# A causal convolution on TensorE: other buffers for the results of the first two steps, and one mid weight by ScalarE and an accumulating DMA

## The chip, the cores and the metric

The kernel runs on one core of a Trainium2 chip. The metric is the device time of one execution in microseconds (us). The kernel before took 785.68 us (median of three runs, 783.73 to 785.83). The profiled execution took 783.4 us, of which the profile covers a span of 781.4 us. All times in views of the profile count from the start of that span.

## The reference

The reference is a causal convolution over time with a full matrix for each tap. x has shape 8 x 4096 x 512 (batch, time, features), the kernel has 8 taps of 512 x 512, and everything is float32.

```
out = np.zeros_like(x)
for k in range(K):                       # K = 8
    shifted = x if k == 0 else concatenate([zeros(B, k, D), x[:, :-k, :]], axis=1)
    out += np.matmul(shifted, kernel[k])
```

So each output row is the sum of eight products of a row of x (the present one and its seven predecessors) with a matrix.

## The kernel before

**Tiling.** The 32768 rows are cut into 128 runs of 256 rows, one run for each partition. A step takes 8 rows of each run, so there are 32 steps (`NIT`). x is loaded in halves of four rows (`load_x(i, h)`, GpSimd's DMA queue, float32 cast to bf16 into two buffers `xin`) and brought into the transposed form that TensorE needs in `XT`. In the steady part this is done by a DMA transpose (`transpose_x`, SyncE's queue), in the first two steps partly by TensorE (`transpose_pe`).

**Fewer products.** Eight outputs from eight taps would take 64 products of a 128 x 512 tile with a 512 x 512 matrix. The kernel splits taps and rows into halves three times. Each half is LO or HI, and a third combination, MID, uses the difference of the two weights and serves both halves. The weights lie in tiles `W[a, b, c]`, all named `w`. The eight loaded ones have no MID in their index; the others are differences formed on the way, by `mid_dve(level, u, v)`, a VectorE subtraction of 128 x 2048 elements in bf16. The sums of x rows that stand opposite these weights are formed by VectorE in tiles whose names begin with D (`D1`, `D2`, `D4`, `D41`, `D42`, `D421`, ...).

**Nodes.** The unit of work is a node: a step i and an outermost index a. A node has nine products (`product`, four matmuls each, L190): `node_a1`, `node_a0`, `node_u`, two `node_v`, four `node_l`. Between them ScalarE and VectorE carry partial sums from one PSUM tile to the next: `node_seed` (L249, L251: ScalarE copies, one negated), `node_dts` (L255, ScalarE), `node_d` (L265 and L76, VectorE). The last part, `node_e`, takes a finished pair of rows (128 x 1024, float32) out of PSUM. For a MID node this is a ScalarE copy into a tile `ms` (L292), the mid sum; for LO and HI nodes it is a VectorE addition or subtraction of the mid sum, into a tile `y`, followed by a store on SyncE's queue (`store`, L275).

**The first two steps** go in another order, since the weights are still being loaded: (0, LO), (1, LO), (0, HI), (1, HI), (0, MID), (1, MID), numbered 0 to 5. Node 0 is computed without differences, by sixteen products `direct(m, t)`. The results of nodes 0 to 3 are copied by ScalarE (L288) into buffers, where they wait for the mid sums: `node_y` (VectorE) adds the mid sum of node 4 or 5 into them in place, and then they are stored. These buffers come from the pools of the later steps: `y` with four tiles, `ms` with two, and `f` with two. From node 6 on, each step has nodes MID, LO, HI in this order.

**What sets the order.** The schedule is written by hand: each engine executes its instructions in the order in which the program text names them, and the program text of the first two steps is one long list (L337 to L559). Waits between engines follow from which tiles are read and written. A tile of a pool with n buffers is taken again for the (n+1)-th request, and the new writer waits for everything that used the old content, a store too.

Of the kernel before, what the change touches and what calls it, by code (L numbers as in the profile page):

```python
# [18 lines left out]
LO, HI, MID = 0, 1, 2  # L19
# [3 lines left out]
def kernel(  # L23
# [6 lines left out]
    nc = tc.nc  # L30
# [10 lines left out]
    ADD = mybir.AluOpType.add  # L41
# [14 lines left out]
    W = {}  # L56
# [11 lines left out]
    D21 = spool.tile([P, 4, D], bf, name="D21")  # L68
# [3 lines left out]
    F0 = spool.tile([P, D], bf, name="F0")  # L72
    A1 = spool.tile([P, 2, D], bf, name="A1")

    def tt(o, a, b, op):
        nc.vector.tensor_tensor(out=o, in0=a, in1=b, op=op)  # L76


    def load(out, src):
        nc.gpsimd.dma_start(out=out, in_=src)  # L80
# [3 lines left out]
    def load_x(i, h):  # L84
        xin[i, h] = xpool.tile([P, 4, D], bf, name="xin")
        load(xin[i, h], xr[:, K * i + 4 * h:K * i + 4 * h + 4, :])

    def transpose_x(i, h):
        nc.sync.dma_start_transpose(
            out=XT[:, 4 * h:4 * h + 4, :].rearrange("p j (c m) -> p (j c) m", m=P),  # L90
            in_=xin[i, h].rearrange("p j d -> p (j d)"))
# [20 lines left out]
    def prep_d41(h):  # L112
        if h == LO:
            tt(D41[:, 0:2], D4[:, 7::-7], D4[:, 0:2], ADD)
        else:
            tt(D41[:, 2:4], D4[:, 3:5], D4[:, 4:6], ADD)
# [7 lines left out]
    def prep_d421(h):  # L124
        if h == LO:
            tt(D421[:, 0:4:2], D42[:, 7:0:-6], D42[:, 0:4:2], ADD)
            tt(D421[:, 1:4:2], D42[:, 0:4:2], D42[:, 1:4:2], ADD)
        else:
            tt(D421[:, 4:8], D42[:, 3:7], D42[:, 4:8], ADD)
# [5 lines left out]
    def pair(k):  # L135
        return ppool.tile([P, 2, D], f32, name=f"pp{k}")
# [4 lines left out]
    H, HF = XT, D421.bitcast(f32).rearrange("p (t b) d -> p t (b d)", b=2)  # L141
# [6 lines left out]
    def load_w(tap):  # L148
        n = K - 1 - tap
        load(W[n >> 2, n >> 1 & 1, n & 1], kr[:, :, tap, :])  # L150

    def mid(level, u, v):

        if level == 0:
            return W[MID, u, v], W[HI, u, v], W[LO, u, v]
        if level == 1:
            return W[u, MID, v], W[u, HI, v], W[u, LO, v]
        return W[u, v, MID], W[u, v, LO], W[u, v, HI]

    def mid_dve(*which):  # L160
        o, u, v = mid(*which)
        tt(o, u, v, SUB)

    load_w(4)
    load(H[:, 1:4], xr[:, RUN - 7:RUN - 4, :])
    ident = spool.tile([P, P], bf, name="ident")
# [8 lines left out]
    def transpose_pe(name, k, src, t0, t1):  # L175
        o = pair(k).bitcast(bf).rearrange("p a (b d) -> p (a b) d", b=2)
        for t in range(t0, t1):
            for c in range(DC):
                nc.tensor.transpose(o[:, t - t0, c * P:(c + 1) * P], src[:, t, c * P:(c + 1) * P],  # L179
                                    ident)  # L180
        bank[name] = o[:, 0:t1 - t0]
# [3 lines left out]
    XF = D42  # L185


    def product(bank, comp, w, start):
        for c in range(DC):
            nc.tensor.matmul(bank, lhsT=comp[:, c * P:(c + 1) * P], rhs=w[:, c, :],  # L190
                             start=start and c == 0, stop=c == DC - 1,
                             skip_group_check=True)

    mpool = ctx.enter_context(tc.tile_pool(name="m", bufs=2))
    cpool = ctx.enter_context(tc.tile_pool(name="c", bufs=2))
    fpool = ctx.enter_context(tc.tile_pool(name="f", bufs=2))
    ypool = ctx.enter_context(tc.tile_pool(name="y", bufs=4))
# [31 lines left out]
    def node_a1(k):  # L229
        n = Node()  # L230
        nodes.append(n)
        n.k, (n.i, n.a) = k, order[k]
        a = n.a
        n.s = streams(n.i, a)
        n.q = pair(3)
        product(n.q[:, 1], n.s[1][1], W[a, MID, HI], True)
        nc.scalar.copy(out=n.q[:, 0], in_=n.q[:, 1])  # L237
        n.p = {}
# [4 lines left out]
    def node_u(n):  # L243
        product(n.q[:, 1], n.s[0], W[n.a, MID, MID], False)

    def node_seed(n, b_):
        n.p[b_] = pair((2 * n.k + b_) % 3)
        if b_ == LO:
            nc.scalar.copy(out=n.p[b_][:, 1], in_=n.q[:, 1])  # L249
        else:  # L250
            nc.scalar.mul(out=n.p[b_][:, 1], in_=n.q[:, 1], mul=-1.0)  # L251
# [8 lines left out]
    def node_d(n, b_):  # L260
        p = n.p[b_]
        if b_ == LO:
            tt(p[:, 0], n.dts, p[:, 1], SUB)
        else:
            nc.vector.scalar_tensor_tensor(out=p[:, 0], in0=p[:, 1], scalar=-1.0,  # L265
                                           in1=n.dts, op0=MUL, op1=SUB)

    ms = {}

    def node_l(n, b_, j):  # L270
        product(n.p[b_][:, j], n.s[3][2 * b_ + j], W[n.a, b_, j], False)

    def store(i, a, b_, y):
        t0 = K * i + 4 * a + 2 * b_
        nc.sync.dma_start(out=orr[:, t0:t0 + 2, :], in_=y)  # L275
# [7 lines left out]
    def node_e(n, b_):  # L283
        p = n.p[b_]
        if n.k < 4:
            pool, name = ((ypool, "y"), (mpool, "ms"), (ypool, "y"), (fpool, "f"))[n.k]
            y = pool.tile([P, 2, D], f32, name=name)
            nc.scalar.copy(out=y, in_=p)  # L288
            first[n.i, n.a, b_] = y
        elif n.a == MID:  # L290
            ms[b_] = mpool.tile([P, 2, D], f32, name="ms")
            nc.scalar.copy(out=ms[b_], in_=p)  # L292
        else:
            y = ypool.tile([P, 2, D], f32, name="y")
            if b_ == HI and n.k == len(order) - 1:

                for j, eng in enumerate((nc.scalar, nc.sync)):
                    tt(y[:, j], p[:, j], ms[b_][:, j], ADD if n.a == LO else SUB)
                    eng.dma_start(out=orr[:, K * n.i + 4 * n.a + 2 * b_ + j, :], in_=y[:, j])
            else:  # L300
                tt(y, p, ms[b_], ADD if n.a == LO else SUB)
                store(n.i, n.a, b_, y)
# [12 lines left out]
    def direct(m, t):  # L315
        n = K // 2 - 1 - m
        product(n0.p[t // 2][:, t % 2], D4[:, t - m] if t >= m else E4[:, 4 + t - m],
                W[LO, n >> 1, n & 1], m == 0)


    C0, C1 = W[MID, HI, MID], W[MID, LO, MID]

    def to(z):
        return z.rearrange("p t (c m) -> p t c m", m=P)[:, :, :, 1:P]

    def prev(z):
        return z.rearrange("p t (c m) -> p t c m", m=P)[:, :, :, 0:P - 1]

    def first_run(z):

        nc.vector.memset(z[:, :, 0:D:G], 0.0)
# [2 lines left out]

    nc.vector.tensor_copy(out=H[:, 4:6], in_=HF[:, 0:2])  # L337
    nc.scalar.copy(out=H[:, 6:8], in_=HF[:, 2:4])
    n0.p = {0: pair(0), 1: pair(1)}
    load_w(6)  # L340
# [21 lines left out]
    load_x(1, 0)  # L362
    tt(to(E4[:, 1:4]), prev(bank["he"]), to(XF[:, 1:4]), ADD)
    direct(2, 2)
    direct(0, 1)
    first_run(E4[:, 1:4])
    direct(1, 1)
    tt(D1, XF[:, 3:5], XF[:, 4:6], ADD)
    mid_dve(1, LO, HI)
    nc.vector.tensor_copy(out=F0, in_=XF[:, 4])  # L370
    mid_dve(2, LO, HI)
    tt(F21, D2[:, 0:4], D2[:, 1:5], ADD)
    direct(2, 0)
# [5 lines left out]
    direct(2, 3)  # L379
    mid_dve(2, LO, MID)  # L380
    direct(1, 0)
    transpose_pe("x1", 2, xin[0, 1], 0, 4)
    nc.vector.tensor_copy(out=XT[:, 4:8], in_=bank["x1"])  # L383
    tt(D4[:, 4:8], XF[:, 4:8], XT[:, 4:8], ADD)
    direct(1, 2)
    tt(D42[:, 3], D4[:, 1], D4[:, 3], ADD)
    transpose_pe("x2", 2, xin[1, 0], 0, 4)
    prep_d41(HI)
    direct(3, 2)
# [10 lines left out]
    tt(D41[:, 1], T4[:, 0], T4[:, 1], ADD)  # L400
    load_w(3)
    node_a1(1)
    direct(2, 1)
    node_u(nodes[1])
    tt(D41[:, 0], D4[:, 7], T4[:, 0], ADD)
    tt(T42[:, 0:2], D4[:, 6:8], T4[:, 0:2], ADD)
# [2 lines left out]
    mid_dve(1, HI, HI)  # L409
    load_w(1)  # L410
    node_e(nodes[0], 0)
    load_x(1, 1)
    load_x(2, 0)
# [8 lines left out]
    node_seed(nodes[1], 1)  # L422
    mid_dve(1, HI, LO)
    node_e(nodes[0], 1)
    mid_dve(2, HI, HI)
    node_v(nodes[1], 1)
    mid_dve(2, HI, MID)
    node_l(nodes[1], 0, HI)
    load_x(2, 1)
    node_d(nodes[1], 1)  # L430
    prep_d421(HI)
    mid_dve(0, HI, HI)
    node_a1(2)
    node_l(nodes[1], 0, LO)
    node_e(nodes[1], 0)
    transpose_x(1, 1)
    node_a0(nodes[2])
# [24 lines left out]
    node_u(nodes[3])  # L462
    node_seed(nodes[3], 0)
    node_l(nodes[2], 1, HI)
    mid_dve(0, HI, LO)
    node_seed(nodes[3], 1)
    tt(D421[:, 0:4], D42[:, 3:7], D42[:, 4:8], ADD)
    node_e(nodes[2], 1)
# [14 lines left out]
    node_dts(nodes[4])  # L483
    tt(D21[:, 2:4], C1[:, 0:2], C1[:, 2:4], ADD)
    mid_dve(2, MID, MID)
    tt(D21[:, 0:2], C0[:, 0:2], C1[:, 0:2], ADD)
    tt(A1[:, 1], C1[:, 0], C1[:, 1], ADD)
    load_x(3, 0)
    transpose_x(2, 0)
    mid_dve(2, MID, LO)  # L490
    node_e(nodes[3], 0)
# [148 lines left out]
```

## Time and profile before

| | before |
|---|---|
| time, median of 3 | 785.68 us |
| span of the profile | 781.4 us |
| TensorE busy | 761.4 us (97%) |
| VectorE busy | 659.6 us (84%) |
| ScalarE busy | 281.9 us (36%) |
| GpSimd busy | 41.3 us (5%) |
| one VectorE subtraction of weights (128 x 2048 bf16) | 1218 ns, 19 of them |
| one ScalarE copy of 128 x 2048 bf16 (L394) | 1912 ns |
| load of half a step of x, issue to landing | 5.7 us median |
| store of a `y` tile / of an `ms` tile, issue to landing | 3.4 / 8.4 us median |

Busy time of PE is modelled at the ends of matmuls, and shapes of one line are averaged unless they are kept apart. Because the steady part from step 2 on repeats every three nodes (23.3 us), views of the first 110 us have to be read by themselves: averages over the span say nothing of them. In the views, `pp` are the PSUM tiles, PE is TensorE's matmul, PEld its weight load, DVE is VectorE, ACT is ScalarE, POOL is GpSimd and SPq is the queue of SyncE. L76 is the line of a helper through which all VectorE additions and subtractions run; they are told apart by their tiles. An arrow with a line in brackets names what ended the wait just before the instruction.

### The profile page before, as it was taken

To read this page: it belongs to the slowest core of one execution; us is meant where nothing else is said; L and a number is where in the kernel's file an instruction comes from. 1 tells how busy PE (TensorE), PEld (TensorE's weight loads), DVE (VectorE), ACT (ScalarE), POOL (GpSimd) and SP (SyncE) were. 2 spreads that over 40 slices of the span, in tenths; PEclk is the share of its full clock that TensorE was granted. 3 is DMA by queue.
4 is the path that set the end of the run, shared out by engine and by line. 5 is a ranking of instruction groups with operands and counts; after the bars stand their busy time and mean duration, and the time that the engine had idled before them with its cause. 6 is when DMAs were issued, how large, how long until landed. Compare 5 with 4: busy or idle time off the path is not lost.

```text
span 781.4 us, 9358 instructions
## 1 busy us (share of the span) xinstructions
PE 761.4 (97%) x3505; PEld 346.3 (44%) x3576; DVE 659.6 (84%) x768; ACT 281.9 (36%) x460; POOL 41.3 (5%) x79
## 2 busy tenths in 40 slices
PE   7899899999999999999999999999999999999997
PEld 3444344444444444444444444444444444444443
DVE  4999888888888888888898888888888898888895
ACT  2453333333333333333323343333333333343332
POOL 4000000000000000000000000000000000000000
PEclk9999999999999999999999999999999999999999
DMA  9974878776877787777687787778797867678843
GB/s 200 211 122 137 203 178 207 159 193 163 184 170 195 177 189 170 181 181 195 155 198 173 174 186 191 190 163 181 167 193 185 195 164 183 167 189 181 203 133 123
DMA packets 159230, 138.90 MB, mean 178 GB/s; under 512 B 130129, under 2 KB 134225, under 8 KB 159057
## 3 DMA queue, kind: packets, MB, share of 16 engines
q1 hardware_dynamic: 145456, 99.89, 45.6%
q0 software_dynamic: 13584, 38.15, 30.8%
q8 instruction: 28, 0.46, 0.2%
q10 hardware_dynamic: 144, 0.26, 0.1%
q14 instruction: 18, 0.14, 0.1%
HBM read 77.33 MB, written 67.11 MB: 185 GB/s over the span
## 4 chain that ended last, share of the span: by engine, by line
PE 90%; DVE 4%; DMA 3%; issue 1%; POOL 1%; ACT 0%; DVEq 0%; ACTq 0%; POOLq 0%
PE pp L190 90%; DMA xin<-in_x_dram 2%; DVE D L76 1%; DVE w L76 1%; DMA out_dram<-ms 1%; DVE y L76 1%; POOL w L80 0%; DVE pp L76 0%; DVE pp L265 0%; ACT pp L249 0%; DVE F L76 0%; DVE XT L383 0%; DVE ms L76 0%; DVE f L76 0%; PE pp L179 0%
## 5 line engine op out<-in xcount | busy, mean ns | idle before, releaser
L190 PE MATMUL pp<-w,D 128*128 128x512 bf16 x3212 | 712.0, 379 | 10.4 <-ACT pp L249 3.0
L190 PEld LDWEIGHTS <-D 128*128 128x128 bf16 x3280 | 320.2, 98 | 395.4 <-issue 5.8
L76 DVE TENSOR_TENSOR D<-D 128x1024 bf16<-128x1024 bf16 (+1 forms) x252 | 228.4, 946 | 1.4 <-ACT D L346 1.2
L76 DVE TENSOR_TENSOR y<-pp,ms 128x1024 f32<-128x1024 f32 (+1 forms) x121 | 146.5, 1211 | 46.4 <-PE pp L190 44.9
L76 DVE TENSOR_TENSOR D<-XT 128x2048 bf16<-128x2048 bf16 (+2 forms) x153 | 142.3, 945 | 10.5 <-DMA XT<-xin 8.5
L237 ACT COPY pp<-pp 128x512 f32<-128x512 f32 x95 | 54.1, 570 | 255.1 <-PE pp L190 252.3
L249 ACT COPY pp<-pp 128x512 f32<-128x512 f32 x95 | 54.2, 570 | 170.9 <-PE pp L190 161.7
L76 DVE TENSOR_TENSOR pp<-dts,pp 128x512 f32<-128x512 f32 x95 | 65.5, 690 | 46.5 <-ACT dts L255 42.8
L292 ACT COPY ms<-pp 128x1024 f32<-128x1024 f32 x60 | 61.0, 1017 | 37.1 <-PE pp L190 30.9
L80 POOL DMA_DIRECT2D xin<-in_x_dram x64 | 34.1, 533 | 690.3 <-DMA XT<-xin 675.7
L265 DVE SCALAR_TENSOR_TENSOR pp<-pp,dts 128x512 f32<-128x512 f32 x95 | 65.8, 693 | 3.3
L255 ACT COPY dts<-pp 128x512 f32<-128x512 f32 x95 | 57.5, 605 | 2.0 <-PE pp L190 2.0
L251 ACT ACTIVATE pp<-pp 128x512 f32<-128x512 f32 x95 | 56.0, 590 | 0.8 <-DVE ms L76 0.8
L190 PE MATMUL pp<-w,XT 128*128 128x512 bf16 x118 | 30.5, 379 | 0.1
L76 DVE TENSOR_TENSOR w<-w,w 128x2048 bf16<-128x2048 bf16 x19 | 22.8, 1218 | 1.3 <-DMA w<-in_kernel_dram 1.2
L190 PEld LDWEIGHTS <-XT 128*128 128x128 bf16 x120 | 11.7, 98 | 14.2
L190 PE MATMUL pp<-w,w 128*128 128x512 bf16 x36 | 9.0, 379 | 0.7 <-ACT pp L249 0.7
L190 PE MATMUL pp<-w,F 128*128 128x512 bf16 x36 | 8.9, 379 | 0.0
L173 PE MATMUL pp<-zero 128*128 128x512 bf16 x15 | 6.2, 575 | 1.2 <-DVE zero L145 1.2
L390 ACT COPY XT<-pp 128x1024 bf16<-128x1024 bf16 x1 | 1.0, 1012 | 17.4 <-PE pp L179 17.4
L80 POOL DMA_DIRECT2D w<-in_kernel_dram x8 | 6.0, 756 | 3.9 <-DMA w<-in_kernel_dram 2.8
L190 PEld LDWEIGHTS <-w 128*128 128x128 bf16 x36 | 3.5, 98 | 5.0 <-issue 1.2
(53 smaller groups left out, 65.8 us busy)
## 6 DMA issues: line engine op xcount, KB each, us to landing
out_dram<-y SPq DMA_DIRECT2D x123, 512.0 KB, 3.4
xin<-in_x_dram POOLq DMA_DIRECT2D x64, 512.0 KB, 5.7
w<-in_kernel_dram POOLq DMA_DIRECT2D x8, 512.0 KB, 17.5
D<-in_x_dram SPq DMA_DIRECT2D x1, 1024.0 KB, 4.8
out_dram<-ms SPq DMA_DIRECT2D x2, 512.0 KB, 8.4
out_dram<-f SPq DMA_DIRECT2D x2, 512.0 KB, 8.8
XT<-xin SPq DMA_TRANSPOSE x61, 6.1
XT<-in_x_dram POOLq DMA_DIRECT2D x1, 384.0 KB, 10.5
```

The costliest lines, as they stand in the source:

```text
L76: nc.vector.tensor_tensor(out=o, in0=a, in1=b, op=op)
L80: nc.gpsimd.dma_start(out=out, in_=src)
L173: nc.tensor.matmul(pw[:, h], lhsT=zero[:, 0:P], rhs=zero, start=True, stop=True)
L190: nc.tensor.matmul(bank, lhsT=comp[:, c * P:(c + 1) * P], rhs=w[:, c, :], start=start and c == 0, stop=c == DC - 1, skip_group_check=True)
L237: nc.scalar.copy(out=n.q[:, 0], in_=n.q[:, 1])
L249: nc.scalar.copy(out=n.p[b_][:, 1], in_=n.q[:, 1])
L251: nc.scalar.mul(out=n.p[b_][:, 1], in_=n.q[:, 1], mul=-1.0)
L255: nc.scalar.copy(out=n.dts, in_=n.q[:, 0])
L265: nc.vector.scalar_tensor_tensor(out=p[:, 0], in0=p[:, 1], scalar=-1.0, in1=n.dts, op0=MUL, op1=SUB)
L292: nc.scalar.copy(out=ms[b_], in_=p)
L390: nc.scalar.copy(out=XT[:, 0:2], in_=bank["x2"][:, 0:2])
```

## The change

There are three groups of edits, all in the part before the loop over the steps.

1. The results of nodes 0 to 3 go into other buffers: node 0 (step 0, LO) into `ms`, node 1 (step 1, LO) into `y`, node 2 (step 0, HI) into `f`, node 3 (step 1, HI) into `y`. The purpose is that the buffers of the mid sums are those whose content is stored first, before node 6, the first to write a mid sum into `ms`, asks for them.
2. Work in the prologue is moved: the cast of two head rows `H` from VectorE to ScalarE; the copy `F0` earlier; the product `direct(2, 1)` from behind the first product of node 1 to a place ahead of the second group of transposes; two VectorE additions change places.
3. The mid weight W[MID, HI, LO] = W[HI, HI, LO] - W[LO, HI, LO] is no longer a VectorE subtraction. ScalarE writes the negated LO weight into the tile, and a DMA on GpSimd's queue adds the HI weight to it in place.

```diff
+    def mid_neg(u, v):
+        nc.scalar.mul(out=W[MID, u, v], in_=W[LO, u, v], mul=-1.0)
+
+    def mid_acc(u, v):
+        nc.gpsimd.dma_start(out=W[MID, u, v], in_=W[HI, u, v], accum_op=ADD)
...
-            pool, name = ((ypool, "y"), (mpool, "ms"), (ypool, "y"), (fpool, "f"))[n.k]
+            pool, name = ((mpool, "ms"), (ypool, "y"), (fpool, "f"), (ypool, "y"))[n.k]
...
-    nc.vector.tensor_copy(out=H[:, 4:6], in_=HF[:, 0:2])
+    nc.scalar.copy(out=H[:, 4:6], in_=HF[:, 0:2])
     nc.scalar.copy(out=H[:, 6:8], in_=HF[:, 2:4])
...
     direct(2, 2)
+    nc.vector.tensor_copy(out=F0, in_=XF[:, 4])
     direct(0, 1)
...
     mid_dve(1, LO, HI)
-    nc.vector.tensor_copy(out=F0, in_=XF[:, 4])
     mid_dve(2, LO, HI)
...
     direct(1, 0)
+    mid_neg(HI, LO)
     transpose_pe("x1", 2, xin[0, 1], 0, 4)
...
     tt(D42[:, 3], D4[:, 1], D4[:, 3], ADD)
+    direct(2, 1)
     transpose_pe("x2", 2, xin[1, 0], 0, 4)
...
     node_a1(1)
-    direct(2, 1)
     node_u(nodes[1])
...
     load_x(2, 1)
+    mid_acc(HI, LO)
     node_d(nodes[1], 1)
...
     node_l(nodes[2], 1, HI)
-    mid_dve(0, HI, LO)
     node_seed(nodes[3], 1)
...
-    tt(D21[:, 0:2], C0[:, 0:2], C1[:, 0:2], ADD)
     tt(A1[:, 1], C1[:, 0], C1[:, 1], ADD)
     load_x(3, 0)
+    tt(D21[:, 0:2], C0[:, 0:2], C1[:, 0:2], ADD)
```

## The prediction

> **What bounds the kernel now.** I began with the busy times of the page: TensorE is the engine to save time on, so an edit pays only where it closes a gap in PE.
>
> ```profile
> PE 761.4 (97%) x3505; PEld 346.3 (44%) x3576; DVE 659.6 (84%) x768; ACT 281.9 (36%) x460; POOL 41.3 (5%) x79
> ```
>
> The span is 781.4 us, so all of PE's gaps together are 20 us. The table by stage (length, then busy us and instructions of each engine, clock, DMA share, GB/s) says where they lie.
>
> ```profile
> 0.00:24.60 24.60, 17.40 (x97) 8.06 (x98) 13.87 (x18) 5.25 (x5) 9.03 (x18) 1.00 1.04 203
> 24.60:38.10 13.50, 12.28 (x77) 6.22 (x80) 12.32 (x18) 8.76 (x10) 1.08 (x2) 1.00 1.20 208
> 38.10:52.70 14.60, 14.13 (x65) 6.27 (x65) 14.60 (x15) 8.81 (x14) 0.53 (x1) 1.00 0.84 141
> ...
> 77.30:86.60 9.30, 6.23 (x29) 2.77 (x29) 8.18 (x10) 2.18 (x4) 0.00 (x0) 1.00 0.97 269
> ```
>
> 7.2 us are lost before 24.6 us, 1.2 and about 0.5 in the next two stretches, and 3.07 in one piece at 83.5 us. The clock is 1.00 throughout. After 90 us the waits name none of PE's. So the whole change has to be read in the first 90 us. For the late gap I took the waits of 78 to 90 us and the timelines of ScalarE and TensorE:
>
> ```profile
> ACT ms L292 <- DMA out_dram<-ms: 5.1, 1, 5.1
> ...
> PE pp L190 <- ACT pp L249: 3.0, 1, 3.0
> ```
>
> The same place in the order of time:
>
> ```profile
> 84.99 1.01 ACT L292 COPY ms<-pp 128x1024 f32<-128x1024 f32 x1 [5.12 <-DMA out_dram<-ms]
> 85.89 0.59 ACT L249 COPY pp<-pp 128x512 f32<-128x512 f32 x1
> ...
> 86.54 10.75 PE L190 MATMUL pp<-w,D 128*128 128x512 bf16 x48 [3.02 <-ACT pp L249]
> ```
>
> ScalarE's mid-sum copy of node 6 (`node_e`) wants an `ms` buffer that still holds result (1, LO, 0), whose store was issued at 76.67 and landed 8.2 us later. It waits 5.12 us; the seeds of node 7 (L249, L251) are queued behind it, and products `v` of node 7 wait for them: 3.02 us of PE.
>
> For the prologue I read the chain that ended last between 24 and 47 us:
>
> ```profile
> 5.94 18.62 DMA xin<-in_x_dram
> ...
> 24.61 1.08 PE pp L179 x16
> ...
> 25.71 1.23 DVE XT L383
> ...
> 30.27 1.15 DVE w L76
> ...
> 41.43 0.61 DVE pp L265
> ...
> 45.35 0.70 DVE pp L76
> ...
> 46.09 0.59 PE pp L190 x2
> ```
>
> Up to 24.56 a load of x ends last; then a nearly unbroken row of VectorE operations up to 46.05; from there PE, with one pass over ScalarE's seeds. So a PE gap filled before 46 us gives nothing unless VectorE's row ends earlier, and a VectorE delay there costs.
>
> **What the Trainium skill says.** "DMA: Bandwidth & Descriptors", section "Issuing engines are not separate DMA queues": transfers started from different engines run on the same DMA engines and interleave. The trace agrees: between 44 and 58 us hardware and software queues take 27.7% and 45.4% of the same 16 engines. "Collectives: The Full Stack", section "The bandwidth ceiling", says that an added-in transfer costs not by its addition but by two source reads. No run here shows that yet. "Perfetto Trace Analysis", section "Optimizing Scalar/DVE Operations", advises handing work to ScalarE where VectorE is saturated; VectorE is at 14.60 of 14.60 us in 38.1 to 52.7, where one of its operations goes away.
>
> **The change part by part.**
>
> *Buffers of the first results.* Results of step 0 LO move to `ms`, those of step 1 LO and both HIs to `y` and `f`. The two `ms` tiles are then stored by the sites at L517 and L533. Their stores are issued at 66.48 and 72.27, and the `y` stores there take at most 5.8 us to landing: both tiles are free by about 78, and the copy of node 6 comes at 79.8 (L237 at 79.29 plus its issue distance 0.5). The 5.12 us go. PE's next limit: product `u` of node 7 ends at about 81.8, seeds take 0.5 each, so L249 ends by 82.4, ahead of 83.5 where PE wants it. Removed: 3.02 us.
>
> The late stores now lie in `y`, first reused by the output of node 7, at 91.92 now and 88.9 after; the tile stored at 76.67 lands at 84.9: 4 us of slack. The other three follow later, each with more.
>
> What the freed time runs into: VectorE is busy to 85.5, so node 7's `node_d` starts there and ends at 86.2; PE needs it at 83.5 + 16 matmuls of 0.216 = 87.0. Then `prep_m` moves to 90.0, while the DMA transpose it reads, issued at 83.78, took 7.4 us: 91.2. VectorE will wait some 1.2 us. I cost this at nothing, because the waits after 90 us show the same wait seven times with PE never waiting:
>
> ```profile
> DVE D L76 <- DMA XT<-xin: 8.5, 7, 1.8
> ```
>
> *direct(2,1) ahead of the second transposes.* It fills the 0.45 us in which PE waits for L383. direct(1,2) begins at about 25.51 (three of its four matmuls are recorded, from 25.73), so the two products end at 25.51 + 8 x 0.216 = 27.24, and the transposes, at 26.99 now, start 0.25 later. ScalarE's copies of them follow, the second ending at 30.01 now and 30.26 after; T4 on VectorE (30.19 now) then starts at 30.31: 0.12 us added to the row that sets the end. PE's own 0.2 gained is lost in that. Bounds: 0 if later distances in the row take it up, 0.35 if the product starts as late as the record says. I take +0.1.
>
> *Cast of H by ScalarE, F0 copied earlier.* VectorE loses a cast of 0.91, ScalarE gets one of 1.05, so the second head transposes come 0.5 to 1 us later. Nothing: direct(0,0) waits till 11.42, ScalarE's copies in between (7.21 to 10.67) have 1 us of room, and what follows is bound by loads up to 24.56. F0 (0.29) moves in front of work that ends before VectorE's wait for a weight, until 18.48.
>
> *The late mid weight.* VectorE loses one subtraction, 1.14 us at 49.42. ScalarE gets a negation; the like-sized copy L394 takes 1.91 us, in its idle 17.41 us ahead of 28.08. But the row after 46 us is PE's: node 3's `node_d` cannot come before its product `v` (53.8), so mid_dve(1, MID, LO) starts near 55.3 rather than 55.49, and the subtraction saves PE nothing.
>
> The accumulating DMA is the unknown. GpSimd issues it right after this load:
>
> ```profile
> 44.34 0.53 POOL L80 DMA_DIRECT2D xin<-in_x_dram  x1 [15.45 <-DMA XT<-xin]
> ```
>
> So it is issued near 44.9, its 512 KB behind a load that lands after 6.3 us at 50.6, and beside a transpose landing at 47.18 + 5.2 = 52.4. First reader: mid_dve(1, MID, LO), with d and seeds of node 4 queued behind it on VectorE; its result feeds a0 of node 4 on PE at 56.97, about 57.1 after. With 1.2 us for the subtraction it must land by 55.75. Estimates of its own time: from the anatomy section of the DMA page (2.0 us plus bytes at 436 GB/s), 3.2 us for 512 KB and 4.4 for two reads. The nearest row, a load of 1 MB read and 512 KB written with little beside it, moved data for 3.2 us and landed 5.0 after its issue. Data of the load ahead ends near 49.6; 3.2 us of its own and 1 to 1.9 shared with the transpose put landing at 54.0 to 55.2. I take 55: no wait that reaches PE. If the adding halves the rate, it is 58.
>
> **Sum**: -3.02 + 0.1 + 0 = -2.9 us; 785.68 - 2.9 = 782.8 (span about 778.5).
>
> **The rivals.**
> 1. *The accumulating DMA is late* by 1 to 2.5 us: PE waits at a0 of node 4, near 57 us, and that isn't caught up. For: an operation no trace shows, sharing engines at 0.8 load. Against: the two-read estimate above. Time 782.8 + 1.0 to 2.5, about 784.5: within 0.3%.
> 2. *The removed wait is replaced*: the late `prep_m` (1.2 us), or a store of the first results slower than 8.2 us, passes through VectorE to PE. For: VectorE is busy 10.54 of 10.80 us in 97.4 to 108.2. Against: the seven harmless waits above. Time at most 782.8 + 1.2 = 784.0, no change.
> 3. *Slower*: the adding runs at a quarter of the load's rate, 12.8 us of its own: landing near 64, 8 us late: 782.8 + 8 = 791. For: only that it is unmeasured. At half rate (58) it would still be 785, so slower needs about 61.
>
> **How the numbers follow.** Forecast 0.75, rival 1 0.13, rival 2 0.05, rival 3 0.07. The forecast is 0.37%, near the 0.3% limit, and the three runs before spread over 2.1 us: a quarter of its share I count as no change. Faster 0.75 x 0.75 = 0.56 and some of rival 2, 0.57; slower 0.07 and a little noise, 0.08; same 0.35. Range: below, 2 us for the spread of runs, 781.0; above, the end of rival 1, 785.6.
>
> **What would show it.** Right: no wait of L292 on an `ms` store; PE without a gap at 83.5; a VectorE wait near 90 us on the transpose with PE unmoved; T4 near 30.3; the add-in landed by 55.7. Wrong: PE idle near 57 us behind the subtraction of `w`, a landing time of the accumulating transfer above 10.8 us, or a new wait of the seeds of node 7.

## The result and the profile after

The changed kernel takes 780.5 us (median of four, 780.2 to 781.85), the kernel before 785.41 us on the same chip: ratio 0.9945, 95% interval 0.9926 to 0.9964. The ratio is one of means; that is 0.55% faster where 0.37% was forecast. The span of the profiled execution went from 781.4 to 778.2 us. So there are two numbers to explain: 3.2 us by the profiles, and some 4.9 us by the medians.

The stage table after, in the stages shown of before (length, then busy us and instructions of each engine, clock, DMA share, GB/s):

```profile
0.00:24.60 24.60, 16.63 (x101) 8.04 (x102) 12.75 (x17) 8.01 (x7) 8.95 (x18) 1.00 1.03 204
24.60:38.10 13.50, 12.18 (x79) 6.14 (x78) 12.64 (x18) 8.67 (x10) 1.08 (x2) 1.00 1.20 208
38.10:52.70 14.60, 14.19 (x66) 6.23 (x64) 14.49 (x16) 8.91 (x14) 1.43 (x2) 1.00 0.86 144
...
77.30:86.60 9.30, 9.30 (x45) 4.17 (x43) 9.27 (x13) 3.16 (x5) 0.00 (x0) 1.00 0.88 271
```

PE is now busy for the whole 9.30 us of the stage in which it was busy for 6.23; in the two stages from 24.6 to 52.7 us its busy time is within 0.1 us of what it was. The late stretch in the order of time:

```profile
80.63 1.01 ACT L299 COPY ms<-pp 128x1024 f32<-128x1024 f32 x1 [1.10 <-PE pp L197]
...
82.36 0.57 ACT L256 COPY pp<-pp 128x512 f32<-128x512 f32 x1 [0.71 <-PE pp L197]
...
83.44 5.14 SPq L89 DMA_TRANSPOSE XT<-xin  x1
...
90.69 1.82 DVE L76 TENSOR_TENSOR D<-XT 128x1024 bf16<-128x1024 bf16 x2 [1.07 <-DMA XT<-xin]
```

(Lines moved by 7: L299 is the mid-sum copy that was L292, L256 and L258 the seeds, L197 the products.) The copy waits 1.1 us for TensorE's product and not for a store; the seed ends at 82.93, ahead of 83.5. The two `ms` tiles were stored at 66.14 and 71.95 and were free by 75.7. The slow store is still there: the first of node 1's results is stored at 76.34 and lands 8.6 us later, where it took 8.2 before, but it now lies in a `y` tile for which nobody asks until 88.40. VectorE waits 1.07 us for the transpose before `prep_m`, where I had put 1.2, and PE runs through: product `u` of node 9, which reads XT, starts at 96.89.

The accumulating transfer, from GpSimd's timeline and the issue table of 40 to 60 us (KB each, median us from issue to landing):

```profile
44.80 0.89 POOL L169 DMA_DIRECT2D w<-w  x1
```

It landed 8.8 us after issue, as this line of that table has it:

```profile
w<-w POOLq DMA_DIRECT2D x1, 512.0 KB, 8.8
```

So it landed at 53.6. Its first reader starts at 55.16; VectorE had other work till then, so it waits for nothing.

### The profile page after: what moved, and what is told of

Its sections match the earlier page's. It is cut to its first block, busy times and chain, and to the rows that moved or that the text cites. A ratio compares the mean times of both kernels' runs of the same rounds, so it can differ in the third digit from the quotient of the medians.

```text
span 778.2 us, 9434 instructions
## 1 busy us (share of the span) xinstructions
PE 763.8 (98%) x3576; PEld 346.3 (44%) x3576; DVE 657.7 (85%) x766; ACT 284.6 (37%) x462; POOL 42.1 (5%) x80
## 4 chain that ended last, share of the span: by engine, by line
PE 91%; DMA 3%; DVE 3%; issue 1%; POOL 1%; ACT 0%; DVEq 0%; SPq 0%; ACTq 0%; POOLq 0%
PE pp L197 91%; DMA xin<-in_x_dram 2%; DVE w L76 1%; DVE D L76 1%; DMA XT<-xin 1%; DVE y L76 1%; POOL w L80 0%; PE pp L186 0%; DVE pp L76 0%; DVE pp L272 0%; ACT pp L256 0%; ACT XT L401 0%; POOL xin L80 0%; DVEq L643 0%; POOL XT L80 0%
## 5 line engine op out<-in xcount | busy, mean ns | idle before, releaser
L197 PE MATMUL pp<-w,D 128*128 128x512 bf16 x3280 | 715.9, 379 | 4.1 <-DMA w<-in_kernel_dram 2.5
L197 PEld LDWEIGHTS <-D 128*128 128x128 bf16 x3280 | 320.4, 98 | 392.2 <-issue 3.0
L244 ACT COPY pp<-pp 128x512 f32<-128x512 f32 x95 | 54.1, 570 | 254.5 <-PE pp L197 254.4
L256 ACT COPY pp<-pp 128x512 f32<-128x512 f32 x95 | 54.2, 570 | 172.7 <-PE pp L197 169.4
L299 ACT COPY ms<-pp 128x1024 f32<-128x1024 f32 x60 | 61.0, 1016 | 33.0 <-PE pp L197 33.0
L258 ACT ACTIVATE pp<-pp 128x512 f32<-128x512 f32 x95 | 56.0, 589 | 0.8 <-DVE y L76 0.8
L197 PE MATMUL pp<-w,XT 128*128 128x512 bf16 x120 | 30.8, 379 | 0.0
L197 PEld LDWEIGHTS <-XT 128*128 128x128 bf16 x120 | 11.7, 98 | 14.2
L197 PE MATMUL pp<-w,w 128*128 128x512 bf16 x36 | 9.2, 378 | 1.3 <-ACT pp L244 0.7
L197 PE MATMUL pp<-w,F 128*128 128x512 bf16 x36 | 8.9, 379 | 0.0
L197 PEld LDWEIGHTS <-w 128*128 128x128 bf16 x36 | 3.5, 97 | 5.8 <-issue 2.1
```

## The experiments

The executions of one kernel differ in the granted clock, of which each has its mean on record; spans below are of single executions. "Stand" is a stretch in which TensorE has nothing to execute.

**1. The buffer names alone**, on the kernel before:

```diff
-            pool, name = ((ypool, "y"), (mpool, "ms"), (ypool, "y"), (fpool, "f"))[n.k]
+            pool, name = ((mpool, "ms"), (ypool, "y"), (fpool, "f"), (ypool, "y"))[n.k]
```

> The kernel before with the four buffer names alone exchanged. My theory (the late wait on the store of a first result is nearly the whole gain): no wait of the mid-sum copy of node 6, no gap of TensorE at 83.5 us, span 781.4 - 3.0 = 778.4 us, ratio to before near 0.996. Rival (the other two groups of edits carry a part of their own, since the timed gain of 4.9 us is larger than the 3.2 us by which the span shrank): span as well near 778.4, but the timed ratio clearly nearer to 1 than that of the full change, 0.9945.

Measured: 780.34 us, ratio 0.9944 (0.9931 to 0.9957), span 778.5. From its waits of 20 to 110 us and TensorE's timeline:

```profile
ACT ms L292 <- PE pp L190: 2.2, 2, 1.1
...
77.58 20.03 PE L190 MATMUL pp<-w,D 128*128 128x512 bf16 x90
```

The mid-sum copy waits for TensorE alone, and TensorE runs through. The four names give the whole gain that can be measured. The rival, that the other edits make up the excess over 3.0 us, falls: the excess is here too.

**2. The full change with the old names** (the same diff, reversed):

> The full change with the old four buffer names. My theory: the copy of node 6 waits again some 5 us for the store, TensorE stands near 83 us for about 3.0, span 781.2 us, ratio to before 0.9995 to 1.000. Rival (the rest of the change carries 1 to 2 us): ratio 0.998 or less.

Measured: 785.85 us, ratio 1.0011 (1.0000 to 1.0022), span 784.1 in the profile. The wait is back, with a longer stand: the products ahead of it end 0.47 us sooner than in the kernel before (83.04 against 83.51), while ScalarE's copy gets its buffer no sooner (85.18 against 84.99). And the profile of this kernel shows what that of the kernel before does not. Its waits from 20 to 110 us, and then its stages (columns as above):

```profile
ACT ms L299 <- DMA out_dram<-ms: 5.8, 1, 5.8
PE pp L197 <- ACT pp L256: 4.3, 2, 3.7
```

```profile
83.00:86.00 3.00, 0.04 (x1) 0.00 (x0) 2.04 (x4) 0.82 (x1) 0.00 (x0) 1.00 1.02 411
87.00:90.00 3.00, 3.00 (x9) 1.08 (x8) 0.70 (x1) 0.69 (x2) 0.00 (x0) 0.51 0.90 129
90.00:92.00 2.00, 2.00 (x10) 0.83 (x8) 1.93 (x3) 0.00 (x0) 0.53 (x1) 0.88 0.13 28
```

TensorE stands for 3.69 us, and after it the clock is 0.51 for three microseconds: nine matmuls in 3.00 us, where at full clock there are fourteen (0.216 apart). In shorter stretches the clock is 0.50 from 87.05 to 90.46, 3.41 us, which at half clock costs about 1.7 us. PE is "busy" all the while: only the clock column and the count of matmuls show it. The Trainium skill, "TensorE: Matmul & The Clock Gate", Part 1, says that after an idle window of some 3.4 us TensorE goes to half clock, until it has been busy for as long. The 3.41 us of half clock after this stand of 3.69 agree; the profiled execution of the kernel before, with a stand of 3.02, has none. Run 11 will show half clock after a stand of only 3.20 us, shorter than the page's window; there the measurement counts, and the last section says what the traces tell of it.

**3. The late weight again on VectorE**, the rest of the change kept:

```diff
-    mid_neg(HI, LO)
...
-    mid_acc(HI, LO)
...
+    mid_dve(0, HI, LO)
     node_seed(nodes[3], 1)
```

> The full change, but the late mid weight again as a subtraction by VectorE (no negation, no accumulating transfer). My theory: TensorE loses between 52 and 62 us the 0.24 us that it gained there in the full change, because the weights of node 4 come later; span 778.4 us. Rival (the subtraction was hidden altogether, as I forecast): 778.2, and TensorE's times from 52 to 62 us as in the full change. A second rival, that the transfer disturbs others by sharing the DMA engines: below 778.0.

Measured: 780.04 us, ratio 0.9940 (0.9925 to 0.9955), span 778.9 at clock 0.994, others at 1.0 778.2. From PE's matmuls after the seeds of node 3 to node 5's first product it takes 8.92 us (53.03 to 61.95) here and before, and 8.68 in the full change (52.56 to 61.24). The two timelines, first of this run, then of the full change:

```profile
53.03 6.27 PE L197 MATMUL pp<-w,D 128*128 128x512 bf16 x27 [0.35 <-ACT pp L258]
...
61.95 1.03 PE L197 MATMUL pp<-w,A 128*128 128x512 bf16 x4
```

```profile
52.56 6.20 PE L197 MATMUL pp<-w,D 128*128 128x512 bf16 x28 [0.35 <-ACT pp L258]
...
61.24 1.03 PE L197 MATMUL pp<-w,A 128*128 128x512 bf16 x4
```

So VectorE's freed subtraction does give 0.24 us in this stretch, as expected here and not as in the prediction. It can't be told in the time, nor in the spans at clock 1.0 (778.2 here, 778.0 and 778.2 in the full change).

**4. and 5. The transfer late.** In the first form its issue was moved behind the load of x (3, 0):

```diff
-    mid_acc(HI, LO)
...
     load_x(3, 0)
+    mid_acc(HI, LO)
```

> The full change with the accumulating transfer issued behind the next load of x instead of ahead of it. My theory (its landing has a deadline near 55.7 us, and what it misses is not caught up): issue near 53.4, 8.8 us to landing, 62.2; the first subtraction that reads it then starts at 62.2 instead of 55.2, TensorE stands for 6 to 7 us before product a0 of node 4, span 784.5 to 785. Rival (the slack behind it takes much of it up, as VectorE's wait of 1.07 us near 90 us is taken up): span under 782.

Measured: 781.53 us, span 779.6. This doesn't answer the question, for a reason I had missed: in the program text the subtraction for W[MID, MID, LO] now stands ahead of the addition, so it reads the negated weight without the added term and waits for nothing. Only a later subtraction waited, 1.17 us, and PE 0.49. What it gives is the transfer with more distance to the load ahead of it: the load is issued at 54.38 and lands at 59.28, the transfer is issued at 57.53 and lands 4.5 us later, at 62.03. So the two overlap for 1.75 us; 4.5 us is not the time of the transfer by itself.

In the second form load and transfer were both named ahead of that reader:

```diff
-    mid_acc(HI, LO)
...
     node_l(nodes[3], 1, HI)
+    load_x(3, 0)
+    mid_acc(HI, LO)
     mid_dve(1, MID, LO)
...
-    load_x(3, 0)
```

> The full change, with the accumulating transfer issued behind the next load of x, and both named ahead of the first subtraction that reads the sum, so that it waits. My theory (landing has a deadline near 55.7 us, and what misses it is not caught up): issue near 53, landing near 62, TensorE stands some 6.5 us before product a0 of node 4 and then runs at half clock for about 3.4 us: span 778.2 + 6.5 + 1.7 = 786.4 us, ratio 1.002 to 1.004. Rival (slack later on takes it up): span under 782.

Measured: 789.95 us, ratio 1.0058 (1.0041 to 1.0075), span 789.0. From its timeline, and its stages after the stand:

```profile
53.53 0.88 POOL L169 DMA_DIRECT2D w<-w  x1
...
62.35 1.22 DVE L76 TENSOR_TENSOR w<-w,w 128x2048 bf16<-128x2048 bf16 x1 [7.29 <-DMA w<-w]
...
63.63 3.60 PE L197 MATMUL pp<-w,D 128*128 128x512 bf16 x8 [6.78 <-DVE w L76]
```

```profile
64.00:66.00 2.00, 2.00 (x6) 0.76 (x5) 2.00 (x4) 0.45 (x1) 0.00 (x0) 0.50 0.00 0
66.00:68.00 2.00, 2.00 (x6) 0.73 (x5) 1.97 (x3) 0.88 (x2) 0.00 (x0) 0.50 0.00 0
68.00:70.00 2.00, 2.00 (x8) 0.73 (x7) 0.64 (x1) 1.30 (x3) 0.00 (x0) 0.64 0.00 0
70.00:72.00 2.00, 2.00 (x11) 0.92 (x10) 0.93 (x2) 1.13 (x3) 0.00 (x0) 1.00 0.00 0
```

Landing, wait and stand are as expected; the span is 2.6 us longer than the 786.4 expected. The half clock lasted nearly 6 us after the stand and not 3.4, and product `u` of node 9 starts 9.5 us later than in the full change (106.43 against 96.89): 6.8 of standing and the rest half clock. Two later waits of PE for VectorE, 1.2 us together, come on top. The profiled execution is the longest of four (787.2 to 789.0). The miss of a deadline on this path is not caught up, and to node 9 it costs 1.4 times the stand.

**6. A plain copy in place of the addition** (one mid weight lacks its second term):

```diff
-        nc.gpsimd.dma_start(out=W[MID, u, v], in_=W[HI, u, v], accum_op=ADD)
+        nc.gpsimd.dma_start(out=W[MID, u, v], in_=W[HI, u, v])
```

> The full change with the transfer as a plain copy of the weight, nothing added, so that one mid weight is left without its second term. What the adding costs: if the second read of the accumulating transfer takes its time, the plain copy lands 1 to 2 us earlier than 8.8 us after issue; if the wait behind the load ahead and the shared engines make up the 8.8 us, it lands within 0.5 us of it. The time of the kernel is in both cases that of the full change, 780.5 us, since landing at 53.6 us was early enough.

Measured: 780.64 us (three executions), span 777.8; landing 8.0 us after issue against 8.8, GpSimd's instruction 0.53 us against 0.89. In these two executions the adding costs 0.8 us to landing, 0.36 of it at the issue: between what the two cases said. Most of the 8.8 us is the load ahead. In the full change, in run 4 and in run 5 the transfer lands 2.6 to 2.8 us after that load has landed (53.60 after 50.96, 62.03 after 59.28, 62.33 after 59.67), and in run 5 it took 8.8 us although transposes had only 0.2% of the engines from 53 to 63 us.

**7. direct(2, 1) back**, the rest of the change kept:

```diff
-    direct(2, 1)
     transpose_pe("x2", 2, xin[1, 0], 0, 4)
...
     node_a1(1)
+    direct(2, 1)
```

> The full change with product direct(2, 1) back behind the first product of node 1. My theory: TensorE waits 0.45 us ahead of the second transposes and no longer 0.66 us for ScalarE's copy L244; products of node 1 after its first node_d start at the same time, counted from the first transposes of half (0, 1), to within 0.15 us, since VectorE's row ends last there; span 778.2 +- 0.3, no difference in time. Rival: a gap of TensorE of 0.45 us filled is 0.45 us gained, and this version is 0.4 us longer.

Measured: 781.17 us, ratio 0.9946 (0.9932 to 0.9961), span 778.9. That span is above the range expected, and by itself would speak for the rival; but 0.38 us of the difference to 778.2 stands ahead of the place, in the landing of a load. PE has its gap of 0.45 us before the second transposes, and none at the copy L244. From the first transposes of half (0, 1) to the product after node 1's `node_d` it is 13.48 us (24.83 to 38.31), 13.54 in the full change (24.45 to 37.99). The filled gap gained nothing there: VectorE's row sets the end, and in its old place the product had covered another wait.

**8. The cast and F0 back**, the rest of the change kept:

```diff
-    nc.scalar.copy(out=H[:, 4:6], in_=HF[:, 0:2])
+    nc.vector.tensor_copy(out=H[:, 4:6], in_=HF[:, 0:2])
...
     direct(2, 2)
-    nc.vector.tensor_copy(out=F0, in_=XF[:, 4])
...
     mid_dve(1, LO, HI)
+    nc.vector.tensor_copy(out=F0, in_=XF[:, 4])
```

> The full change with the cast of the head rows again by VectorE and F0 at its old place. My theory: head transposes 0.3 to 0.5 us earlier, direct(0, 0) as before at the landing of its weight (11.4 to 11.7), the first transposes of half (0, 1) unmoved at the landing of their load (24.3 to 24.9), span 778.2 +- 0.3. Rival (the moved cast was worth something): 0.4 us or more longer.

Measured: 780.42 us, ratio 0.9943 (0.9930 to 0.9957), span 778.1. direct(0, 0) starts at 11.33, behind a VectorE instruction as in the kernel before; in the full change it waits for its weight until 11.63. These 0.3 us don't last: the transposes of half (0, 1) start at 24.34 here and at 24.45 in the full change, each time when their load lands. No cost or gain of the edit can be seen.

**9. and 10. The stand filled.** To part the stand from the clock, the kernel before was given matmuls without use in the gap; no wait was taken away:

```diff
         node_l(cur, 1, LO)
+        if k == 6:
+            for _ in range(6):        # 3 in the second run
+                fill(pair(2))
         node_e(cur, 0)
```

> The kernel before, with twelve more matmuls whose result is thrown away, placed ahead of the products v of node 7: TensorE works 2.6 us of the 3 us in which it stands before them, and no wait is taken away. My theory (the gain is larger than the stand of 3.0 us because in most executions TensorE runs at half clock for about 3.4 us after the stand, which costs 1.7 us more): no reduced clock between 83 and 100 us, spans of all executions within 781 to 782, median near 783.7, ratio 0.998. Rival (executions of the kernel before are longer because the store of the first result lands later in them): the spread stays at 782.7 to 786.3, ratio 1.000.

Measured with twelve: 784.9 us, ratio 1.0001 (0.9993 to 1.0009), so the time said the rival. But the twelve took 3.83 us and held back the seeds by 1.51, and PE resumed at 88.06: they lengthened the delay by more than a microsecond. Their executions lie close together, 784.31 to 785.48, where those of the kernel before go from 783.14 to 786.44. In the profiled execution the clock is 1.00 from 80 to 100 us, and its span, 782.9, is the 781.4 of the kernel before plus the 1.5 of the delay: no sign of half clock. To test it in the time, the filler had to be short enough to delay nothing.

> The kernel before with six more matmuls whose result is thrown away in the gap, instead of the twelve of the run before this one, which took 3.8 us and held back ScalarE's seeds by 1.5 us. My theory (after a gap of some length TensorE runs at half clock for a few us, and this is what makes most executions of the kernel before 1 to 2 us longer than its profiled one): six take about 1.9 us and end before the seeds are asked for, the wait for the store is as long as before, about 1.1 us of standing is left, no clock under 1 between 83 and 100 us, spans of all executions 781.2 to 782.0, median about 783.6, ratio 0.998 to 0.999. Rival (the store itself lands later in those executions): the executions spread over 3 us as those of the kernel before, ratio 1.000.

Measured with six: 783.3 us, ratio 0.9987 (0.9976 to 0.9998). Its timelines, around the gap:

```profile
83.20 1.89 PE L173 MATMUL pp<-zero 128*128 128x512 bf16 x6
86.57 13.98 PE L190 MATMUL pp<-w,D 128*128 128x512 bf16 x63 [1.48 <-ACT pp L249]
```

```profile
85.02 1.01 ACT L292 COPY ms<-pp 128x1024 f32<-128x1024 f32 x1 [5.30 <-DMA out_dram<-ms]
```

The store lands as late as ever and the products resume at the same time as before, 86.57 against 86.54; only the stand is shorter, 1.48 us where it was 3.02. Spans, in us, of all executions:

```
six matmuls more   781.0 to 781.4: 10 of 13;  the other three 782.1, 783.2, 784.0
kernel before      780.9 to 781.5:  6 of 25;  the other 19 from 782.5 to 785.8
```

In the kernel before the six executions that are short have a granted clock of 1.0, the others 0.998 or less. (On the other two chips used, 6 of 36 executions have 1.0, with 780.9 to 782.2; the others go from 781.9 to 784.6.) Useless work in the gap makes the kernel faster, so the excess of most executions is not a later store, which the filler would not have mended. Nor does reduced clock make it wherever it lies: four of the ten short executions with six matmuls have a mean clock of 0.996 or 0.997. It hangs on how long TensorE stands, and half clock after the stand, as seen in run 2, is the cause that fits. It is not seen directly: of an unprofiled execution only the mean clock is recorded, not where it was low. Open stay the three long ones with six matmuls.

**11. A further step**, on the full change: both level-0 weights of HI by transfer, issued earlier, and four edits of order:

```diff
+    mid_neg(HI, HI)
     mid_neg(HI, LO)
...
     load_x(2, 0)
+    mid_acc(HI, HI)
+    mid_acc(HI, LO)
...
-    mid_dve(2, HI, LO)
+    node_seed(nodes[1], 0)
     node_a0(nodes[1])
-    node_seed(nodes[1], 0)
...
     node_d(nodes[1], 0)
+    mid_dve(2, HI, LO)
...
     load_x(2, 1)
-    mid_acc(HI, LO)
...
-    mid_dve(0, HI, HI)
...
-    prep_d4(HI)
...
     node_d(nodes[2], 0)
+    prep_d4(HI)
...
-    node_seed(nodes[3], 0)
+    node_seed(nodes[3], 1)
     node_l(nodes[2], 1, HI)
-    node_seed(nodes[3], 1)
+    node_seed(nodes[3], 0)
```

> The full change and five more edits, to see whether VectorE's row before 46 us and ScalarE's seeds are the rest of what can be had: both level-0 mid weights of HI by negation and accumulating transfer, issued right behind the load of x (2, 0); the subtraction for W[HI, LO, MID] moved behind node_d of node 1; that node's first seed named ahead of product a0; the sum D4 of half HI behind node_d of node 2; the two seeds of node 3 exchanged. My theory: TensorE no longer waits 0.66 us for L256 near 36 us nor 0.35 us near 52 us, products of node 2 from l(HI) on start 0.4 to 0.5 us earlier, span 777.3 to 777.8 us against 778.2. Rival: the two transfers hold up the loads and the transpose of half (1, 1), which VectorE needs at 44 us, and the row ends as late as before or later: span 778 or more.

Measured: 785.58 us, ratio 1.0003 (0.9992 to 1.0014), span 784.0: the gain is gone. From VectorE's and TensorE's timelines:

```profile
48.95 1.23 DVE L76 TENSOR_TENSOR D<-XT 128x2048 bf16<-128x2048 bf16 x1 [2.05 <-DMA XT<-xin]
...
50.96 13.28 PE L197 MATMUL pp<-w,D 128*128 128x512 bf16 x51 [3.20 <-DVE D L76]
```

The transpose of half (1, 1), issued at 39.43, lands 9.5 us later beside the two transfers, where in the full change, issued at 39.22, it took 4.5. VectorE goes on with its result at 48.95, where it did at 44.12, and PE stands 3.2 us. So the rival was right, but it is not all. Just before, VectorE had waited 2.04 us for ScalarE's `dts`, since the sum D4 of half HI now stands behind that `node_d`; of the delay the transpose made the last 2.05 us. And after the stand came half clock, 3.41 us of it (51.49 to 54.90). In the stage behind, PE is as busy as in the full change (second line) with fewer matmuls:

```profile
52.70:63.50 10.80, 10.79 (x45) 4.57 (x45) 8.66 (x10) 4.49 (x8) 0.55 (x1) 0.90 0.70 123
```

```profile
52.70:63.50 10.80, 10.80 (x51) 4.80 (x50) 9.71 (x13) 5.88 (x9) 0.55 (x1) 1.00 0.53 92
```

The 13 executions fall into two groups, 781.8 to 782.2 (4) and 783.4 to 784.2 (9), about as far apart as the 1.7 us that one such stretch of half clock costs. The edits were not tried one by one.

## Why the prediction came out as it did

- **The late wait (-3.02 us)**: right in mechanism and place. L299 waits no longer for a store, PE has no gap, the `y` tiles made no wait in their stead. Run 1 shows that this is the measurable gain, run 2 that no gain is left without it.
- **The size of that term was too small.** I put the gain at the stand of the one profiled execution and wrote "The clock is 1.00 throughout", and I took the 2.1 us between the three runs for a spread on both sides, to be laid around the forecast. Most of it belonged to the kernel before: the stand costs most of its executions more than its length, by half clock after it as far as runs 2, 10 and 11 tell. Run 10 halves the stand and leaves the wait, and gains 1.5 us (784.82 to 783.3). With the wait gone too it is 4.4 to 4.6 us (runs 8 and 1). The forecast of 782.8 is thus 2.3 us above the median of 780.5, of which about 1.5 is this; the lower end of the range, 781.0, lies above the median as well. At clock 1.0 the term was right: the spans are then 780.9 to 782.2 before and 778.0 to 778.2 after.
- **What followed the freed time**: right. VectorE's new wait for the transpose is 1.07 us (1.2 forecast), and PE doesn't feel it.
- **direct(2, 1) (+0.1)**: right, +0.06 (run 7). Missed on the way: PE's new wait of 0.66 us at L244, which the product had covered. It cost nothing because VectorE's row ends last, which was the reason given.
- **Cast and F0 (0)**: right within what run 8 can tell.
- **The late weight**: the transfer landed at 53.6, somewhat before the 54.0 to 55.2 that were forecast, so rivals 1 and 3 did not come. That it came so near is in part luck: 1 to 1.9 us of the sum were for sharing with the transpose, and run 5 had the same 8.8 us with next to no transposes beside it. The second read was put at 1.2 us (4.4 less 3.2), and run 6 shows 0.8 for all that the adding costs. Run 5 shows that the deadline behind rival 1 exists. The statement "the subtraction saves PE nothing" was wrong by 0.24 us: I followed only the reader of the new weight, and not the later subtractions behind it on VectorE. The one for W[MID, LO, MID] starts at 59.08 and not 59.41, and from 52 to 62 us TensorE's weight loads wait 0.4 us for subtractions of `w` where they waited 0.9.
- **Rival 2** (replacing wait) did not come: after 90 us PE's waits sum to 0.2 us.

## What to carry to other kernels

When buffers of a steady loop are borrowed for a prologue, give the ones that the loop asks for first to the results that leave first. Here four names made the whole gain, and all the moved work together none that can be measured. Judge a gap in TensorE by the clock behind it as well as by its length, and compare the spans and clocks of all executions with the profiled one, which may be one of the short ones. Before filling a gap or freeing an engine, look which engine's row ends last there. Before adding a transfer, look for the transfer beside it that somebody waits for, and for the load ahead of it.

## What the runs showed that was not expected

After stands of 3.69, 3.20 and 6.78 us (runs 2, 11 and 5) TensorE ran at clock 0.50 for 3.41, 3.41 and nearly 6 us.

The traces tell more of when this happens. In stretches of 0.1 to 0.25 us the clock of run 2 changes at 11.96, 15.37, 87.05, 90.46 and, after the last products, at 783.37 us. These changes are 1, 21, 1 and 203 times 3.41 us apart, and those of runs 1, 5 and 11 lie in such multiples too. So the clock changes on a fixed grid, and a stand has to be laid against the grid. The window of 3.41 us that ends where the clock falls held 3.10 us of the stand in run 2, 2.88 in run 11 and 2.33 in run 5. In the profiled execution of the kernel before, the clock falls only after the last products, at 781.08; 204 windows earlier a border lies at 84.76, inside the stand (83.51 to 86.54), which is so split into 1.25 and 1.78 us. This would be why that execution kept its clock with a stand of 3.02 while run 11 lost it with 3.20. It is worked out from these traces and was not tested: for unprofiled executions the place of the grid is not recorded. In run 5 the clock fell at 59.18, during the stand, and rose at 69.42, three windows later; only the last of them was full of matmuls.

Reduced clock at the start of the program costs less than it does behind a late stand. Run 1's profiled execution, at half clock from 11.97 to 18.79, has a span of 778.5 us, and one of mean clock 1.0 has 778.2; in run 3, with the like stretch, it is 778.9 against 778.2. PE has waits there in any case: up to 24.6 us it is busy for 17.40 us in the kernel before and for 18.97 in run 1. One unprofiled execution of the full change with mean clock 0.994 has 779.7, and where its clock was low is not recorded.

Six useless matmuls in a gap of 3 us made the kernel before 0.13% faster. An accumulating transfer of 512 KB within SBUF landed in 8.8 us when a load was issued 0.5 us ahead of it, and in 4.5 when the load was 3.2 us ahead.
